# A hybrid decoder layer: extra slots for raw weights in both FFNs, low parts of w_out on VectorE, the residual loaded through GpSimd's queue

## The chip, the cores and the metric

The kernel runs on one core of one Trainium2 chip. The metric is the device time of one execution in microseconds (us). Names of engines: TensorE (PE in the profile; PEld is its weight load), VectorE (DVE), ScalarE (ACT), GpSimd (POOL), SyncE (SP). SP and GpSimd also issue DMAs; an issued DMA waits in its engine's own queue, in program order, until its buffers are free.

## The reference

One layer for 512 prompt tokens and 8 x 4 sample tokens (544 in all), d = 1024, FFN width 2816, all in f32:

```python
x = x + 0.5 * SwiGLU_1(RMSNorm(x))          # gate, up (1024 x 2816), down (2816 x 1024)
z = RMSNorm(x) @ w_in                        # 1024 x 3584, split among two groups of heads
x = x + concat(MoBA(q, k, v), gate * norm(HGRN2(q, f, i))) @ w_out    # w_out 1024 x 1024
x = x + 0.5 * SwiGLU_2(RMSNorm(x))
```

The prompt attends to its own blocks, the samples to a paged cache (gathered page by page through a table). Outputs are both groups' y, the new keys and values, and the recurrent states.

## The kernel before, in words

**Products.** Activations lie transposed, 128 features by 544 tokens a tile, and TensorE works on halves of 272 tokens. To reach f32 accuracy each operand is split in a high part, rounded to f32r, and a low part, the rest; three products (hi x hi, lo of x, lo of w) are added in PSUM (`products`, 702). A weight comes in quarters: a quarter is 512 rows by 128 columns, 256 KB, loaded into a *raw* buffer by SP (`w_load`, 583), then split (`split_unit`, 608): ScalarE copies the high part `whi`; the low part `wlo` is either VectorE's raw - hi (617), or, where `transfer` is set, ScalarE writes the negative of the rounded raw piece and a DMA on GpSimd's queue adds the raw piece onto it (614, 615). In the second case the raw buffer is free only when that transfer is over.

**Plain and paired tiles.** The first `NREG` = 5 hidden tiles of each FFN, w_in and w_out are plain: a tile of 128 output columns is `gemm` (712), two halves of 24 matmuls each. From the sixth hidden tile on (and for down in the second FFN) two weight tiles are multiplied together by a Strassen-like scheme (`paired_gemm`, 739): seven units of 12 matmuls for eight plain ones. Its right-hand factors `xw` are made by `right_factors` (755), and a paired weight job needs five raw pieces, some of them sums made by GpSimd, by accumulating DMAs on its queue or by VectorE (`w_load`, `w_split` 620).

**Buffers.** There are four general raw slots and six pairs of `whi`/`wlo` (1130). `room` (552) gives a slot out; one that was never used comes first. Slots with the mark "a" may only take pieces of paired jobs. `ffn` (960) hands over ten of these raw slots (the no longer needed `xh`, `xl` of tiles 0 to 4) and three weight pairs when it reaches the sixth hidden tile and all `xw` are there (967 to 973), and `fewer_slots` takes them back at the end. `w_pump` (662) splits until `AHEAD` = 4 quarters are ready (`AHEAD_MIX` = 6 while the next job has the mark `mixer`) and loads as long as raw slots are free, in the order of `weight_jobs` (504): first FFN, w_in, w_out, second FFN. That mark is the last argument of `plain` (519): it is set for w_in and w_out, and it also chooses the low part by transfer (652).

**Order.** Nothing is issued while the program is planned. `Order` (258) keeps an estimate of each engine's time; the backbone (`plan`, 1950: `ffn1`, `mix`, `ffn2`) and side chains (attention, recurrence, norm) are stepped by it, each instruction gets an estimated start, and the recorded instructions are given out sorted by that start (`give_out`, 279). A pool's opening and closing cuts the list: what is recorded after it comes after everything before. So every change of a cost or of an engine can reorder instructions.

**Around the end of the mixer.** `mix` (1835) projects with w_in, runs attention and recurrence as chains, and begins the first two output tiles of w_out (1885 to 1898). `ffn2` (1902) then opens its pool in the memory of the mixer's, loads the residual x (spilled to DRAM by `ffn1`) into eight tiles `y` by SP (1906, 1907), and for each of the eight output tiles adds the product to y on VectorE (1913), splits it and takes its squares; GpSimd sums the squares (824). The first two tiles' sums lie in four PSUM buffers; of the `mm` kind there are three. At the end `store` (1928) transposes y, copies it into one of two `yt` tiles and writes it out.

Of the kernel before, what the change touches and what calls it, by code (L numbers as in the profile page):

```python
# [21 lines left out]
KD = D // 128  # L22
# [28 lines left out]
MIXED = (4, 5, 6, 0, 1, 2, 3, 7)  # L51
OVER, TICK, WARM_COLUMNS = 0.0112, 3.413, 3060
NREG = 5
AHEAD = 4
AHEAD_MIX = 6
PACE = 1.1
# [408 lines left out]
class Build:  # L465
# [38 lines left out]
    def weight_jobs(self):  # L504
        a, out = self.a, []

        def quarters(m, nk, r0, c0):
            h = nk // 2
            return [m[128 * r:128 * (r + h), c0:c0 + 128].rearrange("(k p) m -> p k m", p=128)
                    for r in (r0, r0 + h)]  # L510

        def turns(m, nk, r0, c0):
            rows = m[128 * r0:128 * (r0 + nk), c0:c0 + 128].rearrange("(k two p) m -> two p k m", two=2, p=128)
            return [rows[0], rows[1]]

        def job(kind, src, nk):
            out.append({"kind": kind, "src": src, "nk": nk // 2, "raw": [], "done": 0, "paired": kind is not None, "mixer": False})

        def plain(m, nk, r0, c0, mixer=False, start=False):
            job(None, quarters(m, nk, r0, c0), nk)  # L520
            out[-1]["mixer"] = mixer
            out[-1]["start"] = start

        def paired(kind, nk, a11, a12, a21, a22, transfer):
            job(kind, [a11, a21, a21 if transfer else None, a22, a12], nk)
            out[-1]["transfer"] = transfer

        def ffn(p, pairs):
            gate, up, down = (a[p + n][0] for n in ("_gate", "_up", "_down"))
            for g0, ng in FGROUPS[pairs]:  # L530
                for f in range(g0, g0 + ng):
                    if f < NREG:
                        plain(gate, KD, 0, 128 * f, start=True)
                        plain(up, KD, 0, 128 * f, start=True)
                    else:
                        paired("a", KD, *quarters(gate, KD, 0, 128 * f), *quarters(up, KD, 0, 128 * f), pairs)
                for m in range(0, KD, 2):
                    if pairs:
                        paired("a", ng, *turns(down, ng, g0, 128 * m), *turns(down, ng, g0, 128 * (m + 1)), True)
                    else:  # L540
                        plain(down, ng, g0, 128 * m)
                        plain(down, ng, g0, 128 * (m + 1))

        ffn("ffn1", False)
        for n, j in IN_ORDER:
            plain(a["w_in"][0], KD, 0, COLS[n] + 128 * j, True)
        for m in range(KD):
            plain(a["w_out"][0], KD, 0, 128 * m, True)
        ffn("ffn2", True)
        return out  # L550

# [110 lines left out]
    def w_pump(self):  # L662
        def ahead():
            mixer = self.splitting < len(self.jobs) and self.jobs[self.splitting]["mixer"]
            return len(self.units) < (AHEAD_MIX if mixer else AHEAD)

# [293 lines left out]
    def ffn(self, pool, wide, home, x, xg, done, pairs, first=None):  # L960
        nc = self.nc
        self.pairs, self.sums, self.hidden_raw = pairs, wide, (pool, "t_h")
        for g0, ng in FGROUPS[pairs]:
            last = g0 + ng == NFF
            hs = []
            for f in range(g0, g0 + ng):
                if f >= NREG:
                    if f == NREG:
                        yield from self.settle()
                        yield lambda: len(self.xw) == KD // 2  # L970
                        self.more_slots("a", home, [f"{t}{i}" for i in range(5) for t in ("xh", "xl")],
                                        [(f"xh{i}", f"xl{i}") for i in range(5, KD)])
                        self.w_pump()
                    yield from self.paired_gemm(self.xw, KD // 2, self.hidden_paired(pool, f - g0, hs))
                    continue
                gate, up = self.hidden(pool, f - g0, hs)
                if f == 0 and first:
                    for evac, src in zip((gate, up), first):
                        for h in range(2):
                            self.later.append(lambda e=evac, s=src, h=h: e(s[h], h))  # L980
                    continue
                yield from self.gemm(xg, KD, gate, both=f == 0)
                yield from self.gemm(xg, KD, up)
            if pairs:
                for m in range(0, KD, 2):
                    yield from self.paired_gemm(hs, ng // 2, self.down_paired(pool, x, m, done if last else lambda m: None))
                continue
            yield from self.settle()
            if last:
                self.fewer_slots()  # L990
            for m in range(KD):

                def add(p, h, m=m, last=last):
                    c = self.cols(h)
                    nc.vector.scalar_tensor_tensor(x[m][:, c], p, 0.5, x[m][:, c], op0=ALU.mult, op1=ALU.add)
                    if h and last:
                        done(m)

                yield from self.gemm(hs, ng, add, both=m == 0)
        if pairs:  # L1000
            self.fewer_slots()
# [900 lines left out]
    def ffn2(self, xspill):  # L1902
        nc = self.nc
        with self.pool("ffn2") as pool:
            x = [pool.tile([128, T], F32, name=f"y{k}") for k in range(KD)]
            for k in range(KD):
                nc.sync.dma_start(x[k], xspill[k])
            xg = []
            for m in range(KD):

                def add(p, h, m=m):
                    c = self.cols(h)
                    nc.vector.tensor_tensor(x[m][:, c], p, x[m][:, c], op=ALU.add)
                    if h:
                        xg.append(self.split_x(x[m], m, self.gains[:, 2, m:m + 1], pool))
                        self.norm_add(m, x[m])

                if m < 2:
                    for h in range(2):
                        add(self.wo[m][1][h][:, :HT], h)  # L1920
                else:
                    yield from self.gemm(self.mixed, KD, add, self.mix_order)
            self.R = None
            self.order.spawn(self.norm())
            out = self.o["y_prompt"][0].rearrange("(i p) d -> p i d", p=128)
            out_s = self.o["y_sample"].rearrange("b t d -> (b t) d")

            def store(m):
                yield
                y = self.tl(pool, [128, 4, 128], "yt", bufs=2)  # L1930
                ys = self.tl(pool, [NS, 128], "t_s", bufs=2)
                self.to_tokens(x[m], y, ys)
                nc.sync.dma_start(out[:, :, 128 * m:128 * m + 128], y)
                nc.sync.dma_start(out_s[:, 128 * m:128 * m + 128], ys)
                self.stored += 1

            self.stored = 0
            homes = [(self.xp, f"{t}{i}") for i in range(KD) for t in ("xh", "xl")] + [(pool, f"hw{i}") for i in range(5)]
            self.hidden_home, self.staging = lambda i: homes[i], 14
            self.order.spawn(self.right_factors(pool, x, 2))  # L1940
            yield from self.ffn(pool, pool, pool, x, xg, lambda m: self.order.spawn(store(m)), True)
            yield lambda: self.stored == KD

# [40 lines left out]
```

## Time and profile before

| | us |
|---|---|
| median of 3 runs | 1224.61 |
| lowest, highest | 1216.81, 1227.07 |
| the profiled execution | 1221.96 |
| its span, first to last instruction | 1220.2 |
| mean granted TensorE clock | 0.983 |

The rows further below come from the profiled execution. Times in them are us from the start of the span, unless they say ns. A group of operations is named by what it writes and reads: `wlo<-raw,whi` writes a low part. `mm` and `sm` are the two kinds of PSUM buffers. Extra raw slots keep the name of the tile whose memory they use, so `xl<-ffn_gate` is a load of raw gate weights. "[8.93 <-DVE y" is idle time before an instruction and what ended it. All lines of the kernel are issued by one helper, line 288. The granted clock is given as a share of full speed; TensorE has two levels, 1.2 and 2.4 GHz.

### The profile page before, as it was taken

The page shows a single profiled execution, that of the slowest core. Times are in us where ns is not written, and L with a number is a line of the kernel's source. Part 1 is how long each engine was busy: PE and PEld are TensorE (multiplying, and loading weights), DVE is VectorE, ACT ScalarE, POOL GpSimd, SP SyncE. Part 2 cuts the span into 40 slices and gives each one's busy share as a digit, 9 for nine tenths or more (in the row PEclk, how much of TensorE's full clock was granted, in tenths as well). Part 3 has the DMA queues.
Part 4 walks back from the last instruction along what each step waited for, and adds up shares of the span by engine and source line. Part 5 has one row for each costly group of instructions (what it writes and reads, how often), then busy time and mean ns, then how long its engine had stood idle before and what let it go on. Part 6 is the DMA issues. An engine that isn't in the chain of part 4 may idle for free.

```text
span 1220.2 us, 26922 instructions
## 1 busy us (share of the span) xinstructions
PE 1168.5 (96%) x10439; PEld 1102.6 (90%) x10439; DVE 841.2 (69%) x1866; ACT 652.3 (53%) x1369; POOL 329.4 (27%) x358
## 2 busy tenths in 40 slices
PE   8989999999999979999999999699989999998998
PEld 8989999999999978888888777599979999998998
DVE  5877558864775377776576357336958888886896
ACT  6645246632555446665556535255635665665663
POOL 4121021101102541322444456141122223223220
PEclk9999999999999999999999999889999999999999
DMA  6566454453324984855886999464578979969873
GB/s 170 130 165 150 122 152 113 122 145 78 90 64 140 217 225 98 180 125 132 216 234 194 268 308 267 114 174 109 130 180 186 239 168 215 202 133 240 180 164 89
DMA packets 261541, 202.20 MB, mean 166 GB/s; under 512 B 16116, under 2 KB 228628, under 8 KB 261413
## 3 DMA queue, kind: packets, MB, share of 16 engines
q1 hardware_dynamic: 221860, 116.17, 33.1%
q0 software_dynamic: 39456, 84.17, 32.5%
q8 instruction: 82, 1.34, 0.4%
q14 instruction: 47, 0.38, 0.1%
q10 hardware_dynamic: 96, 0.14, 0.0%
HBM read 141.28 MB, written 11.83 MB: 125 GB/s over the span
## 4 chain that ended last, share of the span: by engine, by line
PE 74%; DVE 8%; DMA 7%; issue 4%; ACT 3%; POOL 2%; SPq 1%; POOLq 0%; ACTq 0%; DVEq 0%
PE mm L288 46%; PE sm L288 29%; DMA KV<-cache_v,idx 2%; DVE xl L288 1%; DVE U L288 1%; DMA raw<-w_in 1%; POOL KV L288 1%; DMA wlo<-raw 1%; DMA raw<-ffn_gate 1%; ACT xh L288 1%; DVE xh L288 1%; SPq L288 1%; DMA wlo<-xl 1%; DVE hw L288 1%; DVE xw L288 1%
## 5 line engine op out<-in xcount | busy, mean ns | idle before, releaser
L288 PE MATMUL mm<-xh,whi 128*128 128x272 f32 x948 | 285.4, 303 | 11.9 <-DVE y L288 9.2
L288 PE MATMUL mm<-xl,whi 128*128 128x272 f32 x945 | 272.7, 291 | 3.1 <-DVE xl L288 2.3
L288 PE MATMUL mm<-xh,wlo 128*128 128x272 f32 x912 | 265.2, 291 | 1.2 <-DVE wlo L288 1.2
L288 ACT CAST whi<-raw 128x512 fp32r<-128x512 f32 (+2 forms) x233 | 139.3, 600 | 170.6 <-PE mm L288 106.1
L288 PEld LDWEIGHTS mm<-xh,whi 128*128 128x128 f32 x948 | 180.8, 191 | 28.2 <-issue 13.6
L288 PEld LDWEIGHTS mm<-xl,whi 128*128 128x128 f32 x945 | 180.1, 191 | 4.6 <-DVE xl L288 3.2
L288 PEld LDWEIGHTS mm<-xh,wlo 128*128 128x128 f32 x912 | 174.1, 191 | 1.4 <-DVE wlo L288 1.4
L288 POOL DMA_DIRECT2D wlo<-raw x92 | 83.1, 931 | 225.5 <-ACT wlo L288 186.4
L288 PE MATMUL mm<-hw,whi 128*128 128x272 f32 x737 | 141.3, 288 | 0.8 <-DVE hw L288 0.8
L288 PE MATMUL sm<-xw,whi 128*128 128x272 f32 x648 | 125.0, 291 | 7.7 <-ACT whi L288 5.3
L288 PE MATMUL mm<-xw,whi 128*128 128x272 f32 x648 | 124.3, 290 | 1.0 <-ACT t_g L288 1.0
L288 DVE TENSOR_TENSOR wlo<-raw,whi 128x512 fp32r<-128x512 f32 (+2 forms) x141 | 94.0, 673 | 39.2 <-ACT whi L288 37.2
L288 PEld LDWEIGHTS mm<-hw,whi 128*128 128x128 f32 x737 | 116.0, 188 | 1.7 <-DVE hw L288 1.5
L288 PEld LDWEIGHTS sm<-xw,whi 128*128 128x128 f32 x648 | 102.8, 191 | 8.6 <-ACT whi L288 5.7
L288 PEld LDWEIGHTS mm<-xw,whi 128*128 128x128 f32 x648 | 102.3, 190 | 1.2 <-ACT t_g L288 1.2
L288 PE MATMUL mm<-hw,wlo 128*128 128x272 f32 x358 | 102.9, 287 | 0.0
L288 PE MATMUL sm<-xw,wlo 128*128 128x272 f32 x324 | 94.3, 291 | 0.4 <-DVE wlo L288 0.4
L288 PE MATMUL mm<-xw,wlo 128*128 128x272 f32 x324 | 93.6, 289 | 0.0
L288 PEld LDWEIGHTS mm<-hw,wlo 128*128 128x128 f32 x358 | 67.5, 188 | 0.0
L288 ACT CAST whi<-xh 128x512 fp32r<-128x512 f32 (+2 forms) x84 | 47.2, 566 | 37.7 <-PE mm L288 18.4
L288 PEld LDWEIGHTS sm<-xw,wlo 128*128 128x128 f32 x324 | 62.1, 192 | 0.9 <-DVE wlo L288 0.9
L288 PE MATMUL mm<-xw,xh 128*128 128x272 f32 x304 | 59.6, 292 | 2.4 <-ACT sq L288 2.4
(382 smaller groups left out, 2707.2 us busy)
## 6 DMA issues: line engine op xcount, KB each, us to landing
wlo<-raw POOLq DMA_DIRECT2D x91, 256.0 KB, 4.1
raw<-w_in SPq DMA_DIRECT2D x56, 256.0 KB
raw<-ffn_up SPq DMA_DIRECT2D x43, 256.0 KB
raw<-ffn_gate SPq DMA_DIRECT2D x41, 256.0 KB
xh<-ffn_up SPq DMA_DIRECT2D x32, 256.0 KB
raw<-ffn_down SPq DMA_DIRECT2D x32, 256.0 KB
xl<-ffn_up SPq DMA_DIRECT2D x30, 256.0 KB
xl<-ffn_gate SPq DMA_DIRECT2D x26, 256.0 KB
```

The costliest lines, as they stand in the source:

```text
L288: call(*map(real, args), **{k: real(v) for k, v in kw.items()})
```

## The change

Four edits. (1) `ffn` hands over further raw slots for paired pieces when it starts, not at the sixth hidden tile: four in the first FFN, two in the second, with memory of their own in the pool `wide`. (2) w_out's jobs lose the mark `mixer`: their low parts are made by VectorE, and four quarters instead of six are held ready while they are split. (3) The eight loads of y are issued by GpSimd, not by SP. (4) The tiles that `store` fills are eight, under the names of the first eight right factors, whose memory they share, in place of the two `yt`.

```diff
+NX = {True: 2, False: 4}
...
         for m in range(KD):
-            plain(a["w_out"][0], KD, 0, 128 * m, True)
+            plain(a["w_out"][0], KD, 0, 128 * m)
...
     def ffn(self, pool, wide, home, x, xg, done, pairs, first=None):
         nc = self.nc
         self.pairs, self.sums, self.hidden_raw = pairs, wide, (pool, "t_h")
+        self.more_slots("a", wide, [f"rawx{i}" for i in range(NX[pairs])], [])
...
             for k in range(KD):
-                nc.sync.dma_start(x[k], xspill[k])
+                nc.gpsimd.dma_start(x[k], xspill[k])
...
-                y = self.tl(pool, [128, 4, 128], "yt", bufs=2)
+                y = self.tl(pool, [128, 4, 128], f"xw{m}")
```

`more_slots` (568) appends the slots to the list that `room` searches. The second FFN's down was paired before (`ffn("ffn2", True)`), and stays so.

## Rows read from the trace of the kernel before

**Rows 1.** The page, part 1: busy us of each engine, share of the span, instructions.

```profile
PE 1168.5 (96%) x10439; PEld 1102.6 (90%) x10439; DVE 841.2 (69%) x1866; ACT 652.3 (53%) x1369; POOL 329.4 (27%) x358
```

**Rows 2.** Windows: stretch, busy us (instructions) by engine, granted clock, DMA share, GB/s.

```profile
82.00:94.00 12.00, 7.62 (x46) 6.72 (x45) 6.34 (x8) 4.45 (x10) 4.32 (x4) 0.85 0.73 194
105.00:404.00 299.00, 299.00 (x2376) 297.26 (x2375) 192.99 (x349) 142.62 (x272) 42.80 (x38) 1.00 0.45 121
757.00:770.00 13.00, 9.06 (x140) 6.17 (x139) 9.07 (x27) 3.52 (x15) 3.23 (x4) 0.98 0.66 201
787.00:795.30 8.30, 0.00 (x1) 0.00 (x1) 0.50 (x2) 0.00 (x0) 0.00 (x0) 0.68 0.92 239
795.30:801.00 5.70, 5.70 (x27) 5.70 (x28) 3.06 (x7) 3.21 (x5) 1.40 (x1) 0.56 0.70 247
803.00:833.00 30.00, 30.00 (x242) 30.00 (x241) 10.16 (x19) 16.28 (x29) 13.28 (x13) 1.00 0.67 152
894.00:911.00 17.00, 11.30 (x73) 10.42 (x72) 7.39 (x14) 7.05 (x16) 3.98 (x5) 0.90 1.00 232
1118.00:1135.00 17.00, 14.22 (x99) 13.46 (x98) 9.73 (x20) 8.49 (x19) 3.31 (x4) 0.90 0.90 213
```

**Rows 3.** Timeline of TensorE around 790 (start, us, operation, idle before).

```profile
786.09 0.28 PE L288 MATMUL mm<-xh,wlo 128*128 128x272 f32 x1
795.30 0.59 PE L288 MATMUL mm<-xh,whi 128*128 128x272 f32 x1 [8.93 <-DVE y L288]
```

**Rows 4.** Timeline of SP's queue in the same place.

```profile
783.61 7.17 SPq L288 DMA_DIRECT2D raw<-w_out  x4
791.06 3.87 SPq L288 DMA_DIRECT2D y<-xs  x8
```

**Rows 5.** Timeline of GpSimd there.

```profile
758.99 2.08 POOL L288 TENSOR_TENSOR s<-s,hf 128x512 f32<-128x512 f32 x2
...
784.45 1.73 POOL L288 DMA_DIRECT2D wlo<-raw  x2 [1.85 <-ACT whi L288]
```

**Rows 6.** The chain of waits there (start, us, what).

```profile
785.00 5.34 DMA wlo<-raw
```

**Rows 7.** Timeline of VectorE there: last read of the mixer's tiles.

```profile
775.48 0.72 DVE L288 TENSOR_TENSOR xl<-rec,xh 128x544 fp32r<-128x544 f32 x1
```

**Rows 8.** The chain of waits at the first FFN's switch.

```profile
84.23 3.77 DMA raw<-ffn_gate
```

**Rows 9.** Timelines of SP and TensorE at the second FFN's switch.

```profile
892.29 0.37 SPq L288 DMA_DIRECT2D xl<-ffn_down  x1
...
899.46 0.41 SPq L288 DMA_DIRECT2D raw<-ffn_gate  x1
...
905.53 0.52 PE L288 MATMUL sm<-xw,whi 128*128 128x272 f32 x2 [4.48 <-ACT whi L288]
```

**Rows 10.** Timelines of SP and ScalarE at the last group's start.

```profile
1117.97 0.37 SPq L288 DMA_DIRECT2D xl<-ffn_gate  x1
...
1124.85 0.62 ACT L288 CAST xh<-xl 128x512 fp32r<-128x512 f32 x1 [6.00 <-DMA xl<-ffn_gate]
```

**Rows 11.** Groups by line and shape: low parts (count | busy, mean ns | idle before).

```profile
L288 DVE TENSOR_TENSOR wlo<-raw,whi 128x512 fp32r<-128x512 f32 x108 | 76.4, 715 | 28.5 <-ACT whi L288 26.9
...
L288 POOL DMA_DIRECT2D wlo<-raw x92 | 83.1, 931 | 225.5 <-ACT wlo L288 186.4 <-PE mm L288 15.0 <-DVE xw L288 8.2
...
L288 ACT ACTIVATE wlo<-raw 128x512 fp32r<-128x512 f32 x91 | 57.1, 627 | 0.0
```

**Rows 12.** The page, part 6: low-part transfers (count, size, us to landing).

```profile
wlo<-raw POOLq DMA_DIRECT2D x91, 256.0 KB, 4.1
```

**Rows 13.** Timelines of VectorE and GpSimd near 70.

```profile
71.00 1.18 DVE L288 TENSOR_TENSOR xw<-hw,xw 128x272 fp32r<-128x272 f32 x1
...
70.03 1.85 POOL L288 TENSOR_TENSOR raw<-raw,raw 128x512 f32<-128x512 f32 x1 [3.56 <-DVE wlo L288]
```

**Rows 14.** Tile w_in: who waited for its loads (us, times).

```profile
  ACT whi L288: 13.4, 5
```

## The prediction

> **What bounds the kernel now.** I read the busy shares first. TensorE is busy for 1168.5 of 1220.2 us and no other engine comes near [rows 1], so time can only be won where TensorE stands still or runs at its lower clock. Then I cut the span into stretches and counted matmuls [rows 2]. Between 105 and 404 us, where nothing stalls, 2376 matmuls fill 299 us: 0.126 us each. A stretch is worth its matmuls times 0.126, and the rest of it is lost (busy time hides part of that, since the end of a matmul is modelled 0.29 us after its start):
>
> - 82 to 94: 46 matmuls, 5.8 us of work, 6.2 lost. Start of the paired products of the first FFN.
> - 757 to 770: small products of the mixer, no fixed rate; 13 minus 9.06, so 3.9 idle.
> - 787 to 795.3: nothing at all, 8.3 lost; 795.3 to 801: 27 matmuls, 3.4 of work, 2.3 lost at a granted clock of 0.56. Second and later tiles of w_out.
> - 894 to 911: 73 matmuls, 9.2 of work, 7.8 lost, the clock at 0.90. Start of the paired products of the second FFN.
> - 1118 to 1135: 99 matmuls, 12.5 of work, 4.5 lost, the clock at 0.90. Start of its last group.
>
> The third step was to ask what ended each of these waits.
>
> *The stop before 795.3.* TensorE starts its last matmul at 786.09 and the next at 795.30, released by the residual add into y on VectorE, after 8.93 us idle [rows 3]; by start times the gap is 9.2 minus 0.1, so 9.1 us. The tile for the second half of w_out's third tile is a PSUM buffer that this add must empty. The add waits for y, and the eight loads of y stand in SP's queue behind four loads of raw w_out, which hold the queue from 783.61 until the first y goes out at 791.06 [rows 4]. Those wait for raw buffers, which are still read by low-part transfers on GpSimd's queue: the last two go out at 784.45 [rows 5], and the chain of waits shows 5.34 us of wlo<-raw from 785.00 [rows 6]. So a weight that is needed much later holds up a residual that is needed now. After the stop the clock is at the lower of its two levels (1.2 of 2.4 GHz, granted 0.56 over that stretch), which is the 2.3 us.
>
> *The other three.* In the first FFN the chain of waits runs over a raw<-ffn_gate load, from 84.23 for 3.77 us [rows 8]. At 905.53 TensorE had stood 4.48 us for a high part on ScalarE; its raw ffn_gate went out at 899.46, the eleventh in a row of loads that begins at 892.29 with ten of ffn_down that nobody needs yet [rows 9]. At 1124.85 ScalarE had stood 6.00 us for an ffn_gate load that SP could only issue at 1117.97 [rows 10]. The first two are a late fifth raw piece: a paired job takes five raw buffers, and only four general ones exist until the extra ones are handed over at the sixth hidden tile. The third is a load that waited for any free buffer among all 14.
>
> **The change, part by part.**
>
> *Residual through GpSimd's queue and low parts on VectorE* belong together. Moving y alone would put it behind the same low-part transfers, which are on GpSimd's queue in that place [rows 5]; taking the low parts away alone would free the raw buffers but leave y behind four loads. With both, GpSimd has nothing between its products at 759 to 761 [rows 5] and y. The first y then waits for the mixer's memory. Its last reader that I see is the split of the last rec tile on VectorE, 775.48 plus 0.72, so 776.2 [rows 7]. One issue on GpSimd takes 0.93 us [rows 11] and a 256 KB transfer from that queue lands 4.1 us later [rows 12]: y0 at 781.2, y1 at 782.2, y2 at 783.1, the eighth at 787.7. Two adds of 0.44 us free the buffer by some 783.4, and TensorE wants it at 786.2. Slack 2.8 us, so the 9.1 goes whole, and with the stop goes the low clock: 9.1 + 2.3 = 11.4 us. What is late next there: the adds stand in VectorE's queue behind the low parts of the fourth tile, whose high parts need weight buffers that the first tile frees. Behind that tile come 18 matmuls of the second and 24 of the third, 5.3 us, before 786.2: freed at 780.9, split by some 782.3, still in time. Without the cover each us that y0 comes after 785.3 costs one. Behind the y issues on GpSimd stand only sums of squares, first wanted near 788.
>
> On VectorE 16 low parts of 0.715 us come in, 11.4 us; GpSimd loses 16 times 0.931, ScalarE 16 times 0.627 [rows 11]. From 803 to 833 VectorE is busy 10.2 of 30 us [rows 2], so its share is hidden there. Before 770 it is not clear: the sample attention is late, VectorE works 9.07 of 13 us on it [rows 2], and some four low parts may fall in between, 2.9 us at most; on the other side six transfers leave the queue and the DMA engines that the last gathers use, which can win back up to the 3.9 idle. Take 0, bounds +2.9 and -3.9. The flag that is dropped also lowers the number of split quarters held ahead from six to four. A low part was ready some 5.0 us after its issue (0.93 + 4.1) and is now ready in 0.7, while one tile of 48 matmuls lasts 6.0 us, so four suffice: 0.
>
> The Trainium skill ("SBUF — State Buffer", Who interferes with whom) says that a VectorE operation with two SBUF inputs and a GpSimd operation that reads SBUF shut each other out. The trace bears it out: a 272-column subtraction took 1.18 us at 71.00, while GpSimd's sum of 1.85 us ran, against 0.44 for others [rows 13]. By it the seven sums of squares after 787 could each hold a low part, at most 1.4 us each; VectorE's idle 20 us from 803 to 833 take that, and the total stays.
>
> *Four more raw slots in the first FFN.* They hold only paired pieces, and a slot that was never used is taken first. The plain tiles keep the general four; the loader then puts the first four pieces of the first paired job in the new ones and the fifth in a general one before the switch. So the load of 84.23 goes out before the run of loads at the switch and the 6.2 us shrink to what ScalarE and VectorE still take one after the other, some 0.2: 6.0 won. Bounds 0 (that run keeps the DMA engines full anyway) and 7.3 (with the low clock that lasts beyond 94).
>
> *Two in the second FFN.* The first two pieces of the job take them, the other three take general slots that the last plain tiles free, before the run of ffn_down loads. Of the 7.8 us I take 6.0: the idle 4.48 and about half of the other 3.3; the rest I leave, because the down job behind is then wanted 6 us earlier. Bounds 0 and 7.8. At 1118 two more buffers let SP run two loads ahead; a paired job of 84 matmuls is 10.6 us for five pieces, so two pieces are about 4 us. I take 2.5 of the 4.5 (bounds 0 and 4.5), since a transfer on the same DMA engines still has to fit.
>
> *The output tiles* move from a pair to eight that reuse the right factors' memory. Their last readers, the last paired gate and up products, are over before the last down products begin; 0.
>
> Sum: 11.4 + 0 + 6.0 + 6.0 + 2.5 = 25.9, say 26. The profiled execution took 1221.96 us (span 1220.2, 1.8 around it), 2.65 under the median of 1224.61. 1221.96 - 26 = 1196.
>
> **Rivals.**
>
> *The slots buy nothing.* The pieces come early, but the run of loads behind them is then the late one, so each stop moves by one job. For it: nothing less is loaded in all. Against: TensorE loses nothing from 105 to 404 [rows 2], where paired jobs run with more slots than one job needs. Only the 11.4 remain: 1210.6.
>
> *y isn't early.* It waits for other mixer memory, or its eight transfers meet the w_out loads. For it: the pool is given back whole. Against: nothing is seen of the mixer after 776.2. Then 14.5 remain: 1207.5. The Trainium skill ("DMA: Bandwidth & Descriptors", Issuing engines are not separate DMA queues) speaks for it: all queues end on the same 16 DMA engines, and another issuing engine saves only the time to issue. The wait in rows 4 is one for buffers, not for the DMA engines, so I don't follow it.
>
> *Both fail*, or the new order, which is computed from estimated times, loses elsewhere what is won here: 1212 to 1224, say 1219.
>
> *Slower: VectorE stops at low parts whose raw is late.* Until now nothing on VectorE waited for w_out. Its queue is in order, so a low part whose load is late holds the attention and later the adds and splits behind it. The nearest price: ScalarE's high parts waited 13.4 us in five waits for w_in loads [rows 14], 2.7 each. All 16 would cost 43 us, net +17: 1239. It decides from ten of 16 on (26 / 2.7). Against: the four loads in rows 4 are for the sixth and seventh tile, and TensorE is then at the third; w_out is loaded well ahead.
>
> **How the numbers follow.** Forecast 0.62, slots 0.15, y 0.08, both 0.10, slower 0.05. All stops gone is 7.3 + 11.4 + 7.8 + 4.5 + 3.9 = 35 and some low clock with it, 40 in all: 1182. At the other end the first rival with the 2.9 of VectorE gives 1213.5. Range 1182 to 1214; above lies most of the last two cases. About 1%, 12.2 us, can be told from no change, so the line is 1209.7: the forecast, the y case and somewhat over half of the slots case are faster, 0.79; slower by over 1% takes 14 late low parts, which with odd losses elsewhere I put at 0.05; 0.16 between.
>
> **What would show it.** Right: no idle over 2 us of TensorE where y is added, and y<-xs issued on GpSimd while TensorE works on w_out's second tile; no stop over 1.5 us at the two switches; the fifth piece of the first paired job issued before the switch; w_out's low parts as VectorE operations, 16 fewer transfers from GpSimd. Wrong: y's add again the releaser of a stop of several us; the stops at the switches as long as before with ffn_down or ffn_up as the releaser; VectorE idle behind a high part of w_out.

## The result, and the profile after

| | before | after |
|---|---|---|
| median of 8 runs each, us | 1219.85 | 1210.08 |
| lowest, highest | 1216.81, 1227.07 | 1208.53, 1214.89 |
| the profiled execution | 1221.96 | 1208.81 |
| its span, mean granted clock | 1220.2, 0.983 | 1207.0, 0.993 |

The ratio is 0.9917, with an interval of 0.989 to 0.9943: 9.8 us faster, where 26 were forecast. The median lies half a microsecond from the rival "the slots buy nothing" (1210.6). That it is so near is in part luck: the rival's figure counts from 1221.96, and the median of before is 1219.85 here.

The first part of the page of the kernel after (busy us of each engine, share, instructions), against [rows 1]:

```profile
PE 1163.7 (96%) x10439; PEld 1097.1 (91%) x10439; DVE 854.6 (71%) x1882; ACT 644.4 (53%) x1353; POOL 319.5 (26%) x350
```

VectorE has the 16 low parts of w_out more, ScalarE 16 and GpSimd 8 instructions fewer (16 transfers away, 8 loads of y added). So the change does what it says. Windows of the kernel after: the first three at the times of [rows 2], the fourth 0.7 us before the second FFN's first paired product as there (0.8), the fifth where TensorE now stops near its last group, the sixth on the work of the last row of [rows 2] (from 8.1 us after the last group's first product, there 8.2):

```profile
82.00:94.00 12.00, 9.05 (x58) 8.65 (x58) 8.84 (x13) 6.20 (x14) 4.30 (x4) 0.86 0.87 233
787.00:795.30 8.30, 8.30 (x68) 8.30 (x68) 5.03 (x10) 4.86 (x8) 2.76 (x2) 1.00 0.80 259
795.30:801.00 5.70, 5.70 (x48) 5.70 (x47) 2.99 (x6) 2.43 (x4) 1.35 (x1) 1.00 0.48 138
884.00:901.00 17.00, 11.62 (x87) 11.41 (x86) 8.83 (x19) 7.50 (x18) 6.15 (x7) 0.94 0.97 230
1096.00:1113.00 17.00, 14.22 (x100) 14.00 (x100) 10.87 (x21) 8.06 (x17) 3.49 (x4) 0.90 1.02 224
1108.00:1125.00 17.00, 17.00 (x138) 17.00 (x137) 13.54 (x27) 11.40 (x24) 4.42 (x6) 1.00 1.03 224
```

Read the first count in brackets, the matmuls. In w_out the empty 8.3 us now hold 68, and the slow stretch behind it has 48 at full clock where it had 27. At the first FFN's switch there are 58 for 46, 1.5 us, which the stretch as a whole hardly keeps (below). At the second FFN's switch there are 87 where there were 73: 14 more, 1.8 us, not 6. In the last group the stop of before is gone (138 against 99 on the same work), but a new one stands some 16 us earlier in the work (100 in 17 us), so little is won.

To see where the time goes in every kernel alike, I cut each profiled execution at the starts of nine TensorE operations: the norms' first products, the recurrence's last decay product (the last `sm<-sqsum,hk`), the first product on `xw` of each group of hidden tiles, and the last operation. Starts are those of the timeline's rows, where like operations in a run are one row. Each number is the difference of two such starts, in us. (Both profiles of before and both of after are in it, since a stretch is known no better than two executions of one kernel agree.)

| | before, again (e16) | after, again (e7) | e2 | e13 |
|---|---|---|---|---|
| norm 1 to first paired product | 51.08, 51.07 | 52.51, 52.66 | 51.07 | 51.08 |
| to second group | 89.78, 87.80 | 88.94, 88.41 | 90.15 | 83.66 |
| to norm 2 | 235.92, 236.01 | 235.48, 235.47 | 235.91 | 240.73 |
| to the last decay product | 329.63, 324.75 | 328.93, 326.20 | 328.25 | 328.82 |
| mixer's end, w_out, to norm 3 | 99.38, 99.58 | 90.06, 88.00 | 90.77 | 91.35 |
| to first paired product | 61.12, 61.14 | 61.06, 61.03 | 61.09 | 61.07 |
| second switch, to second group | 52.80, 52.83 | 49.17, 48.71 | 52.49 | 44.99 |
| to third group | 95.55, 96.50 | 96.94, 96.99 | 97.57 | 95.63 |
| to the end | 171.82, 171.97 | 170.79, 170.73 | 171.85 | 171.77 |

The gain is in the row of w_out, 9.3 to 11.6 us. The second switch gives some 3.9, of which the next row takes 1 back; the first FFN gives nothing, and its first row is 1.5 us longer. The mixer's row differs by 5 us between two executions of the same kernel, so nothing is read from it.

*w_out.* The timelines of VectorE and GpSimd in the kernel after, for [rows 5, 7]:

```profile
779.17 0.72 DVE L289 TENSOR_TENSOR xl<-rec,xh 128x544 fp32r<-128x544 f32 x1
...
780.51 4.37 POOL L289 DMA_DIRECT2D y<-xs  x8 [21.11 <-PE mm L289]
785.89 0.78 DVE L289 TENSOR_TENSOR y<-mm,y 128x272 f32<-128x272 f32 x2
```

y waits for the mixer's memory, as the prediction said. (The row names a TensorE product as the last of the twelve semaphores that y waits for. But in all thirteen profiles with both parts the first y goes out 0.62 us after the end of that last split.) The mixer ends 3.7 us later (779.17 against 775.48; in the second profile of after 775.34), so y goes out at 780.51. The eight issues take 0.55 us each, not 0.93. The first add runs at 785.89, and TensorE comes to the freed buffer at 787.57 without a wait.

The row of w_out has two parts that behave differently. From the start of the last split, `xl<-rec`, to norm 3 it is 58.2 and 58.6 us in the two profiles of before and 44.5 in both of after: the stop, the low clock behind it, and 16 products (2.0 us) that are now done before the split (354 matmuls are left after it, where there were 370). From the last decay product to that split it is 41.1 and 41.0 before, but 45.6 and 43.5 after. So w_out itself wins more than the row shows, and the tail of the mixer takes some of it back.

*The first FFN.* Timelines of SP, GpSimd, ScalarE and TensorE, kernel after:

```profile
31.78 0.45 SPq L289 DMA_DIRECT2D rawx<-ffn_gate  x1
32.28 1.05 SPq L289 DMA_DIRECT2D rawx<-ffn_up  x2
...
36.78 1.82 POOL L289 TENSOR_TENSOR rawx<-rawx,rawx 128x512 f32<-128x512 f32 x1 [9.50 <-PE mm L289]
38.89 0.87 POOL L289 DMA_DIRECT2D rawx<-rawx  x1 [0.30 <-POOL rawx L289]
39.48 2.06 POOL L289 DMA_DIRECT2D wlo<-raw  x2
...
46.89 0.62 ACT L289 CAST whi<-raw 128x512 fp32r<-128x512 f32 x1 [3.76 <-DMA raw<-ffn_gate]
...
50.31 0.39 PE L289 MATMUL mm<-xh,wlo 128*128 128x272 f32 x1 [1.15 <-DVE wlo L289]
```

Three paired pieces go out from 31.78 on, 48 us before they are needed. Their sum and their accumulating transfer stand on GpSimd's queue before the low-part transfers of the plain tiles, which in the kernel before go out at 34.88 and 38.72 and now at 39.48 and 40.06. So raw buffers come free late, the next plain load is late (ScalarE waits 3.76), and TensorE stops for 1.15 us at 50.31. That is most of the 1.5 us of the first row, and the same pattern as the stop that the change removes in w_out: a weight that is not needed yet ahead of one that is.

At the switch itself the chain of waits (start, us, what) and the timelines of ScalarE and TensorE read:

```profile
84.05 4.79 DMA rawx<-ffn_up
...
88.92 0.62 ACT whi L289
89.53 0.29 ACT sq L289
```

```profile
88.92 0.62 ACT L289 CAST whi<-rawx 128x512 fp32r<-128x512 f32 x1 [4.37 <-DMA rawx<-ffn_up]
...
89.87 0.65 PE L289 MATMUL mm<-xw,xh 128*128 128x272 f32 x2 [1.79 <-ACT sq L289]
```

The first paired job is in time now. The late load is the fourth piece of the job behind it: it reloads one of the new slots, and SP issues it at 84.05 behind eight loads into the buffers just handed over (77.70 to 82.32). ScalarE waits 4.37 us at its high part, and the copy `sq` behind it in the queue, which TensorE does need, waits with it.

*The second FFN's switch*, SP's timeline and the chain of waits of the kernel after:

```profile
882.05 0.37 SPq L289 DMA_DIRECT2D rawx<-ffn_down  x1
...
886.23 0.45 SPq L289 DMA_DIRECT2D xh<-ffn_down  x1
886.77 1.17 SPq L289 DMA_DIRECT2D raw<-ffn_down  x1
```

```profile
886.77 7.04 DMA raw<-ffn_down
...
894.42 3.25 DMA raw<-xh
...
897.77 0.56 DVE raw L289
898.33 0.53 DVE wlo L289
898.86 0.36 DVE U L289
...
899.26 2.86 PE sm L289 x11
```

```profile
899.26 0.82 PE L289 MATMUL sm<-xw,whi 128*128 128x272 f32 x2 [5.38 <-DVE U L289]
```

Again the paired job's own pieces are early and the 4.48 us of [rows 9] are gone; now a piece of the first down job is late. It goes into a general buffer, and SP issues it at 886.77 right behind nine other loads of ffn_down that it gives out from 882.05 on, most of them, by the order of `w_load`, for later jobs; it takes 7.04 us, and an accumulating transfer has to follow. TensorE waits for U, which is ready to be computed, but stands in VectorE's queue behind a sum for the down job. The stop is 5.38 us where it was 4.48; but it is the only wait of TensorE in that row of the table, where before had six of 6.8 us in all.

*The last group*, chain of waits and TensorE's timeline of the kernel after:

```profile
1092.38 6.88 DMA wlo<-rawx
...
1099.30 0.39 PE L289 MATMUL sm<-xh,wlo 128*128 128x272 f32 x1 [2.25 <-DMA wlo<-rawx]
```

ScalarE's late load [rows 10] is gone, but some 16 us ahead of that place a low-part transfer on GpSimd's queue is late in its stead.

### The profile page after: what moved, and what is told of

The parts are those of the page before. It is cut to its first block, busy times and chain, and to the rows that moved or that the text cites. A ratio compares the mean times of both kernels' runs of the same rounds, so it can differ in the third digit from the quotient of the medians.

```text
span 1207.0 us, 26863 instructions
## 1 busy us (share of the span) xinstructions
PE 1163.7 (96%) x10439; PEld 1097.1 (91%) x10439; DVE 854.6 (71%) x1882; ACT 644.4 (53%) x1353; POOL 319.5 (26%) x350
## 4 chain that ended last, share of the span: by engine, by line
PE 76%; DVE 9%; DMA 8%; ACT 3%; issue 3%; POOL 1%; SPq 0%; POOLq 0%; ACTq 0%; DVEq 0%
PE mm L289 46%; PE sm L289 30%; DVE xl L289 1%; DMA KV<-cache_v,idx 1%; DVE U L289 1%; DMA wlo<-rawx 1%; DMA rawx<-ffn_up 1%; ACT xh L289 1%; DMA xh<-ffn_up 1%; DVE xh L289 1%; DVE wlo L289 1%; DMA xl<-ffn_up 1%; DVE hw L289 1%; DMA raw<-ffn_down 1%; DVE xw L289 1%
## 5 line engine op out<-in xcount | busy, mean ns | idle before, releaser
L289 ACT CAST whi<-raw 128x512 fp32r<-128x512 f32 (+1 forms) x207 | 124.3, 602 | 165.2 <-PE mm L289 112.9
L289 PEld LDWEIGHTS mm<-xh,whi 128*128 128x128 f32 x948 | 178.9, 189 | 15.9 <-issue 13.6
L289 POOL DMA_DIRECT2D wlo<-raw x82 | 75.9, 955 | 178.6 <-ACT wlo L289 138.2
L289 DVE TENSOR_TENSOR wlo<-raw,whi 128x512 fp32r<-128x512 f32 (+2 forms) x125 | 84.4, 681 | 33.9 <-ACT whi L289 32.3
L289 PEld LDWEIGHTS mm<-xw,wlo 128*128 128x128 f32 x324 | 61.7, 190 | 0.3 <-DVE wlo L289 0.3
```

The lines of the kernel that those rows point to most:

```text
L289: call(*map(real, args), **{k: real(v) for k, v in kw.items()})
```

## The experiments

All kernels were compared with runs of the kernel before on the same chip. Intervals are 95%; with half-widths of mostly about 0.003, two kernels are told apart from 4 us on, and below that the table of stretches decides.

**The parts of the change.** e1 is the kernel before with the slots and the output tiles alone:

```diff
+NX = {True: 2, False: 4}
+        self.more_slots("a", wide, [f"rawx{i}" for i in range(NX[pairs])], [])
-                y = self.tl(pool, [128, 4, 128], "yt", bufs=2)
+                y = self.tl(pool, [128, 4, 128], f"xw{m}")
```

> The kernel before with the new raw slots (4 and 2) and the output tiles in the right factors' memory; y stays on SP, w_out's low parts stay transfers. Theory A (the slots buy nothing: each late piece is only exchanged for the next one; the gain of the whole change is that of w_out): within 3 us of before, ratio 0.998 to 1.002, with TensorE still idle for over 2 us at both FFN switches. Theory B (the slots win about 6 us, and the new order loses it again in the mixer once y and the low parts are moved): 5 to 7 us faster, ratio 0.994 to 0.996, or 12 us by the prediction's own sum (0.990).

Measured: 0.9949 (0.9926 to 0.9971). e2 has the other two parts alone:

```diff
-            plain(a["w_out"][0], KD, 0, 128 * m, True)
+            plain(a["w_out"][0], KD, 0, 128 * m)
-                nc.sync.dma_start(x[k], xspill[k])
+                nc.gpsimd.dma_start(x[k], xspill[k])
```

> The kernel before with y on GpSimd's queue and w_out's low parts on VectorE, without the slots. Theory A: the whole gain of the change, 8 to 12 us, ratio 0.990 to 0.993. Theory B: the mixer's end is late in the same way, so about half of it, 4 to 6 us, ratio 0.995 to 0.997.

Measured: 0.9916 (0.9886 to 0.9946). e2 lies where theory A has it, where B's loss in the mixer would have halved the gain (the tail of the mixer is 46.3 us, 5.2 longer than before, but w_out wins more than that); e1 lies where B has it. So neither is whole: y and the low parts are most of the gain, but the slots alone win about 0.5%. By its stretches e1 gains 3.3 us at the second switch (49.47) and loses 2.2 at the start (53.24); the rows beside the mixer's give 1 to 2 us in all, so what else it won in its times isn't located. e3 and e4 split e2:

> y on GpSimd's queue alone; w_out's low parts stay transfers on that queue. The prediction says that y then stands behind the same low-part transfers: 0 to 2 us faster, the stop before the third tile's second half still above 6 us. Rival: the four loads on SP were the whole cause and y gets away in time: stop gone, 8 to 11 us faster.

> w_out's low parts on VectorE alone; y stays on SP. The prediction says that y stays behind four loads of raw w_out, but these wait for buffers that VectorE now frees early, so how much of the stop remains is open: if the order of issues on SP is what holds y, 0 to 3 us faster and a stop of over 5 us; if the low-part transfers were what held SP, the stop goes and it is 8 to 11 us faster (as good as both moves together).

e3, y alone: 0.999 (0.9972 to 1.0008), nothing. e4, the low parts alone: 0.9914 (0.9888 to 0.994), as much as both. The timelines of GpSimd and TensorE in e3, then of SP and TensorE in e4:

```profile
783.83 1.73 POOL L288 DMA_DIRECT2D wlo<-raw  x2 [1.85 <-ACT whi L288]
785.15 4.21 POOL L288 DMA_DIRECT2D y<-xs  x7
...
792.24 0.60 PE L288 MATMUL mm<-xh,whi 128*128 128x272 f32 x1 [6.49 <-DVE y L288]
```

```profile
780.70 7.95 SPq L288 DMA_DIRECT2D raw<-w_out  x3
789.07 4.63 SPq L288 DMA_DIRECT2D y<-xs  x8
...
793.48 0.40 PE L288 MATMUL mm<-xh,whi 128*128 128x272 f32 x1 [0.47 <-DVE y L288]
```

In e3 y stands behind the low-part transfers, exactly as forecast. In e4 y stands behind three loads on SP, goes out 3.9 us after the end of the last split (before: 14.9) and is added late, at 793.0, but TensorE stands only 0.47 us there: it still had products of w_out to do.

From the start of the last split to norm 3 the parts come apart cleanly: 58.2 and 58.6 us before, 55.2 in e3, 45.2 in e4, and 44.5 in each of twelve profiles with both parts (all but e12, whose order differs). So the low parts take away all but 0.7 us, and y adds that 0.7. The whole row of e4 is 93.03 us, more than with both parts (87.6 to 92.3), because its tail, from the last decay product to the split, is 47.8 us. The tail is 43.1 to 47.9 us in the twelve, 42.9 and 43.0 in e1 and e3, and 45.6 and 43.5 in two executions of the same kernel after; why it is longer with the low parts on VectorE, and why it varies, isn't shown. The Trainium skill ("DMA: Bandwidth & Descriptors", Issuing engines are not separate DMA queues) has it that another issuing engine only saves the time of issuing; e3 agrees for y, though what y waits for in its row is the queue ahead of it.

**The slots of each FFN.** e7 is the changed kernel once more, e5 has `NX = {True: 0, False: 4}`, e6 `NX = {True: 2, False: 0}`.

> The changed kernel itself, beside the others on one chip. Theory A (y and the low parts are the whole gain, 8 to 10 us): ratio 0.991 to 0.994. If the slots' gain of the slots-only kernel (0.995) adds to that of y and the low parts (0.992): ratio 0.986 to 0.989, 14 to 16 us faster.

> The changed kernel with the four slots in the first FFN alone (none in the second). The two profiles with slots so far reach the first paired product 1.4 to 2.2 us later after the first norm than four profiles without (51.1 us each), and win that back at the switch: so 0 to 1 us lost by these slots, as fast as y and the low parts alone, ratio 0.991 to 0.994. By the prediction's term they would win 6.0 us more: 0.986 to 0.988.

> The changed kernel with the two slots in the second FFN alone (none in the first). The profiles with slots win 2.3 to 3.4 us between the third norm and the middle of the second FFN: ratio 0.987 to 0.991, 1 to 4 us faster than y and the low parts alone. By the prediction's terms (6.0 + 2.5): 0.983 to 0.986.

Measured on one chip: e7 0.9905 (0.9873 to 0.9937), e5 0.9949 (0.9927 to 0.9972), e6 0.9875 (0.9846 to 0.9904). The changed kernel lies 3.9 us above e6 and 6.2 below e5 (1207.35, 1203.43, 1213.54). So the second FFN's slots win and the first FFN's lose, if anything. e5 lies slightly above the 0.991 to 0.994 expected, and its interval excludes the 0.986 to 0.988 of the prediction's term. e6 lies in the range expected, 0.987 to 0.991. The 6.2 us between e5 and e7 are not all the slots': in the two profiles the second switch holds 4.1 (52.81 against 48.71), and the row of w_out another 4.2, by the tail of the mixer (47.8 and 43.5 us). By stretches, the first takes 52.5 to 53.2 us in five kernels that load the first FFN's new slots early (after, e7, e1, e5, e8) and 51.1 in eight without these slots (before, e16, e2, e3, e4, e6, e9, e11); the second is 88.4 to 90.5 with and 87.8 to 90.9 without; the third is 0.45 shorter with. Net about 1 us lost. e7 lies between its two cases and its interval reaches into both, so it does not say whether the gains add.

**The run of loads.** e8 lets the loader go one job ahead only:

```diff
         job = self.jobs[self.loading]
+        if job["paired"] and self.loading - self.splitting > 1:
+            return False
```

> The changed kernel, but loads of a paired job start only when the job before it is being split, so that the run of 13 ffn_down loads at the second switch is cut to some five at a time. Theory A in its form 'the late piece is slowed by the loads that share the DMA engines with it' (7.04 us for one ffn_down load): the 5.4 us stop at the second switch falls under 2 us and the whole is 2 to 5 us faster than the changed kernel. Theory C (the bytes are the bound there, in whatever order they come): the stop stays over 4 us or moves, within 2 us of the changed kernel, or slower where one job is too little.

Measured: 0.9875 (0.9843 to 0.9907), 3 us under e7, less than the times can tell apart. And the stop stays, 5.60 us, and the trace shows that the edit did not do there what it was to do. SP and TensorE in e8:

```profile
879.84 0.48 SPq L289 DMA_DIRECT2D xl<-ffn_down  x1
...
884.12 1.41 SPq L289 DMA_DIRECT2D raw<-ffn_down  x1
...
896.40 0.82 PE L289 MATMUL sm<-xw,whi 128*128 128x272 f32 x2 [5.60 <-DVE U L289]
```

The same loads run ahead of the same late piece: the loader came to them later, but in the plan a load starts as soon as its buffer and SP's queue have a gap, so it is dated back. What its stretches gain is elsewhere: from the third group to the end 166.80 us in place of 170.7, the stop of 2.25 us at 1099.30 is gone, and the row before it is back at 95.51.

> y, the low parts, two slots in the second FFN alone, and loads of a paired job only one job ahead. If the loss by the first FFN's slots (about 4 us between the runs with and without them) and the gain by one job ahead (about 3 us) are separate: 3 us faster than either alone, ratio 0.983 to 0.986. If one job ahead only repaired what the first FFN's slots spoil: 0.986 to 0.989.

e9 (e8 with `NX = {True: 2, False: 0}`): 0.9864 (0.9837 to 0.9892). It lies at the bound between the two cases, its interval covers both, and it does not tell them apart.

> y and the low parts, no new slots, loads of a paired job only one job ahead. If the run of early loads is what makes the late piece late, one job ahead does without slots what the slots do: switch and first downs of the second FFN (52.4 to 53.5 us without slots, 48.7 to 49.5 with them) under 50 us, ratio 0.985 to 0.989. If buffers are what is short: 52 us and more, ratio 0.990 to 0.995.

e11 (e2 with the limit): 0.9941 (0.9918 to 0.9963), the second switch 54.02 us, the end 174.23. The limit alone does nothing for the switch; buffers are needed too.

**Dating.** e10 keeps loads into the new slots from being dated back:

```diff
+        floor = self.order.floor
+        if x["tags"][0][:4] == "rawx":
+            self.order.floor = max(floor, self.order.free["pe"])
...
         job["raw"].append((raw, x))
+        self.order.floor = floor
```

> The changed kernel, but a load into one of the new slots is dated no earlier than the moment at which the loader comes to it, where the plan so far dates it back to any earlier gap of SP's queue since the slot was never used. Theory: in the first FFN three paired pieces go out at 31.8 us, their sum and their accumulating transfer stand on GpSimd's queue from 36.8 ahead of the low-part transfers that free the raw buffers (39.5 in place of 34.9), and so VectorE and TensorE wait at 50 us. Then the time from the first norm to the first paired product falls from 52.5 to 51.1 us, and the stop of 1.15 us at 50.31 is gone; the rest as the changed kernel, 1 to 3 us faster than it. Rival: the early bytes themselves slow the plain loads, or the slots cost somewhere else: 52.5 stays.

Half a hit: 0.9886 (0.9858 to 0.9913). The stop at 50.31 is gone and GpSimd's low-part transfers are back at 35.35 and 39.19, but the first stretch is 52.68: the pieces, now issued from 54.61 on, put the same sum and transfer before another low part, and TensorE waits 1.27 us at 69.13. e12 instead tells the planner a slower DMA rate (`330e3` to `240e3`):

> The changed kernel, its order planned with 240 GB/s for transfers in place of 330 (the trace shows 234 to 248 GB/s where the DMA share is about 1). If the stops at the switches come from splits and GpSimd work queued for pieces that the plan thinks have landed, the 5.4 us stop of the second switch falls under 3 us and the whole is 2 to 5 us faster than the changed kernel. If not, within 2 us of it, or slower by a new order elsewhere.

A miss: 1.0023 (1.0006 to 1.0039). The last stretch is 167.23 us, but the mixer's end comes in another order (TensorE waits 4.24 us for ScalarE at 764.79 and still waits for paged gathers at 788.01), and the stretch to norm 3 takes 113.50. This is how much an order can cost. (Nor is there one rate at a full DMA share: the windows of 5 us further below, at shares from 0.96 to 1.15, hold 166 to 301 GB/s.)

e13 dates every paired load no earlier than the loader comes to it and keeps the limit; e14 has the dating without the limit; e15 is e10 with the limit. The edit of e14, against e10:

```diff
-        if x["tags"][0][:4] == "rawx":
+        if job["paired"]:
```

> The changed kernel, loads of paired jobs dated no earlier than the loader comes to them and at most one job ahead. If the order of the loads makes the stop of the second switch: the second piece of the first down job goes out ahead of the run of ffn_down loads, lands in some 4 us, and the stop of 5.0 to 5.6 us falls under 2.5 us; switch and first downs (49.2 to 49.5 us with slots) 45 to 47. If the bytes make it: the DMA share stays about 1 from 885 to 905 and the stretch stays 48.5 us or more.

> As e13 without the limit of one job ahead. If the order is the cause, the second switch gains as in e13, and the last group keeps its stop of over 2 us (170 to 171 us from the third group's first product to the end, against 166.8 with one job ahead). If the bytes are: 48.5 us or more at the switch.

> The changed kernel with the new slots' loads not dated back and one job ahead. If the gains add: first norm to second norm 374 to 375 us (376.5 to 376.9 in the changed kernel), the third group to the end 166 to 168, ratio 0.983 to 0.987. If a new order loses it elsewhere: 0.987 to 0.992.

> The kernel before. If the chip sets the mixer's 324 to 330 us, its stretch from the second to the fourth norm lies beside that of e13 to e15 within 1 us; if the change (or the order that comes with it) does, it stays at 329.6. Its whole: ratio 0.998 to 1.002.

e13: 0.9821 (0.9777 to 0.9866), median 1198.89 against 1219.49, the lowest ratio of all, though its interval overlaps those of e6, e8 and e9. e14: 0.9886 (0.9845 to 0.9928). In both the second switch's stop is gone: 44.99 and 44.35 us. SP's timeline in e13, then its windows there, and the windows of the kernel after on the same stretch:

```profile
880.74 1.93 SPq L289 DMA_DIRECT2D raw<-ffn_down  x2
882.76 0.44 SPq L289 DMA_DIRECT2D rawx<-ffn_down  x1
883.29 0.44 SPq L289 DMA_DIRECT2D xh<-ffn_down  x1
```

```profile
885.00:890.00 5.00, 5.00 (x42) 5.00 (x41) 3.93 (x9) 2.95 (x8) 1.75 (x2) 1.00 0.81 226
890.00:895.00 5.00, 5.00 (x42) 5.00 (x41) 2.41 (x5) 2.39 (x7) 2.63 (x3) 1.00 1.15 280
895.00:900.00 5.00, 3.84 (x28) 3.42 (x28) 4.11 (x10) 3.41 (x8) 0.00 (x0) 1.00 1.09 232
```

```profile
885.00:890.00 5.00, 5.00 (x43) 5.00 (x42) 4.23 (x10) 3.41 (x9) 0.86 (x1) 1.00 0.86 223
890.00:895.00 5.00, 3.88 (x32) 3.67 (x30) 0.63 (x1) 1.01 (x3) 0.57 (x1) 1.00 1.05 301
895.00:900.00 5.00, 0.74 (x3) 0.74 (x4) 2.23 (x5) 1.85 (x4) 4.72 (x6) 0.91 0.96 166
```

The general raw buffers' pieces now go out first, at 880.74, and the run into the handed-over buffers follows. The DMA share (last column but one) is 0.81 to 1.15 in e13 and 0.86 to 1.05 after, so full DMA engines alone do not stop TensorE. The order of the loads does: the same bytes in another order pass without the stop.

The first switch clears in e13 as well: one wait of 1.16 us at 82.71 where the kernel after has four, and 83.66 us in the second stretch. But the third stretch is 5 us longer. In e13's windows the loads of the next group, no longer dated back, fill the DMA engines from 150 to 170, and TensorE has 281 matmuls in 40 us where 317 fit (at 0.126 us) and the kernel after has 324; TensorE waits 4.1 us in all there for splits on ScalarE and VectorE:

```profile
150.00:170.00 20.00, 17.95 (x141) 17.50 (x140) 9.11 (x14) 5.51 (x10) 8.19 (x7) 1.00 1.00 274
170.00:190.00 20.00, 17.88 (x140) 17.45 (x140) 16.00 (x26) 12.57 (x25) 5.80 (x6) 1.00 0.63 152
```

e14 loses the same there (240.19) and keeps a stop of 2.74 us in the last group, as expected, though its last row, 171.62, lies outside the 170 to 171 expected and says no more than e13's 171.77, which has the limit and not the 166.8 of e8. e15: 0.9896 (0.9861 to 0.993), the case "loses it elsewhere": its first stretch is 51.07, but ScalarE waits 6.74 us at the first switch and the end takes 175.90. The gains of e8 and e10 did not add here. e16, the kernel before in a single run, took 1216.78 us; its mixer row of 324.75 is as short as in e8 (324.11) and in e14 (322.95), so those short mixer rows are no effect of the edits.

## Why the prediction was wrong in size and right in w_out

**y and the low parts, 11.4 us forecast: right.** The row of w_out falls from 99.4 and 99.6 to 90.1 and 88.0, and e2 alone gives 0.9916. Stop and low clock went together, as the windows show. The step "Moving y alone would put it behind the same low-part transfers" is shown by e3. The other half, that y stays "behind four loads" when the low parts alone are moved, holds for the queue (three loads in e4) but hardly as a cost: 0.7 us. The slack was thinner than forecast: the first add came 5.4 us after the first issue of y and freed its buffer 1.2 us before TensorE came to it, not 2.8. The mixer's tail was taken as 0 between +2.9 and -3.9. In the two profiles of after it is 4.5 and 2.4 us longer; less the 2.0 us of products that moved ahead of the split, it cost 2.5 and 0.4. In other kernels with both parts it cost up to 4.8, beyond the bound.

**Four slots in the first FFN, 6.0 us forecast: wrong, 0.9 us lost.** The step that failed begins with a reading, "The first two are a late fifth raw piece". Timelines of the kernel before, by engine:

```profile
83.67 0.62 ACT L288 CAST whi<-raw 128x512 fp32r<-128x512 f32 x1 [2.43 <-DMA raw<-ffn_gate]
85.28 0.68 DVE L288 TENSOR_TENSOR raw<-raw,raw 128x512 f32<-128x512 f32 x1
88.07 0.62 ACT L288 CAST whi<-raw 128x512 fp32r<-128x512 f32 x1 [3.50 <-DMA raw<-ffn_gate]
88.17 1.26 POOL L288 TENSOR_TENSOR xl<-raw,xh 128x512 f32<-128x512 f32 x1 [14.31 <-DMA raw<-ffn_gate]
89.03 0.52 PE L288 MATMUL mm<-xw,xh 128*128 128x272 f32 x2 [2.45 <-ACT sq L288]
```

The first job's fifth piece is the load before that of 84.23: it is split at 83.67, and at 85.28 VectorE adds the job's first piece onto it. The load of 84.23 ends the wait of GpSimd's sum at 88.17, and such a sum takes the first two pieces of a job (`w_load`): so it is the second job's first piece. Its split at 88.07 stood ahead of `sq` in ScalarE's queue, and TensorE's longest wait, 2.45 us, was for `sq`. So in the main the stop was the next job's already; for the first job's fifth piece TensorE waited 0.96 us, at 84.63. Then "the loader then puts the first four pieces of the first paired job in the new ones and the fifth in a general one before the switch" came true in the kernel after (the fifth went out before 68), but "So the load of 84.23 goes out before the run of loads" doesn't follow. In the kernel after the second job's first two pieces are early too (out by 72.12), its fourth is in the run, at 84.05, and TensorE waits 1.79 us for `sq` in the same way.

The prediction's first rival, the lower bound 0, is near what came. It was rejected with a stretch from 105 to 404, where the loads are spread, while at the switch ten buffers come free at once. That the stop can be taken away is shown by e13 (some 5 us in that stretch), though in e13 the next stretch lost as much. And no step allowed for the loss before the switch: an early load also brings its sum and its transfer early, into GpSimd's queue.

**Two slots in the second FFN, 6.0 and 2.5 us: half right.** The switch gains 3.6 and 4.1 us (52.8 to 49.2 and 48.7), since f5's own wait is gone, but a stop of 5.0 to 5.6 us is back for the down job. The phrase "because the down job behind is then wanted 6 us earlier" saw the place and priced it at the 1.8 us left standing. The last group gives 1.1 of 2.5, since the wait of 2.25 us took the place of the late load, and the row before it lost 0.5 to 1.4.

**The output tiles, 0:** no stop of TensorE was seen at them; they were never tried by themselves.

By these rows, means of two profiles and two, the sum is -10.4, +0.9, -3.9, +0.9, -1.1: 13.6 us beside the 9.8 and 12.7 of the two comparisons. The slots give 3.2 of their 14.5.

## What to carry to other kernels

A buffer more moves a load earlier and the shortage to another one; check first to which job the late load belongs. Before counting a stop as won, follow the load behind it through the same queue, at the moment when many buffers come free at once. An early load also brings its follow-up work early, so look at the queue of the engine that does it. Where engines and DMA queues work in order, which load goes first can be worth more than a further buffer: here some 4 us at the second switch (e13 and e14 against the kernel after), with the same bytes. What it won at the first switch was lost again in the next stretch.

## What the runs showed that was not expected

- A stretch with a DMA share of 1.15 and 280 GB/s went by without any idle TensorE (e13, 890 to 895), and one of 1.05 and 301 GB/s held a stop (after).
- Two executions of the same kernel, in different comparisons, differ by 4.9 us in the mixer (329.63 and 324.75), while stretches without gathers agree within 0.1 (51.08 and 51.07, 52.80 and 52.83).
- After a stop the granted clock can stay high or fall: from 90 to 100 us the two profiles of the kernel before were granted 0.66 (52 matmuls) and 1.00 (68 matmuls), with nearly the same waits before it. The program is the same; the second row of the table differs by 2.0 us.
- The issue of one DMA on GpSimd took 0.55 us for y in the kernel after and 0.93 on average for low parts [rows 11].
